# Retention and latent-attention decoder on one core: unused filler tiles that give all matmul operands the same byte offset modulo 512

## The chip, the cores and the metric

The kernel runs on one core of one Trainium2 chip. The metric is device time in microseconds (us) for one execution, as the median of several runs. A core has five engines that run their own instruction streams: TensorE (PE, matmuls and transposes), VectorE (DVE), ScalarE (ACT), GpSimd (POOL) and SyncE (SP, which issues most transfers). The on-chip memory, SBUF, has 128 partitions; a tile takes the same stretch of bytes in every partition, so a tile's place is one byte offset. Matmul results go to PSUM, which has eight banks of 128 x 512 float32.

## The reference

Two layers act on x, 512 tokens of width 1024, in float32. Layer A is a retention layer of 4 heads (key width 256, value width 512), layer B a latent attention of 16 heads (128 plain and 64 rotary query columns, value width 128) on a compressed key and value stream. Both are gated and end in a DeepNorm step:

```python
# layer A: q, k, v, gate = x @ w_in ; rope(q), rope(k) ; o = retention(q, k, v)
# y = (layer_norm(o) * silu(gate)) @ w_out ; x = LayerNorm(alpha * x + y)
# layer B: lat = rms_norm(x @ w_down) ; k, v = lat @ w_up ; q = rms_norm(x @ w_q_lat) @ w_uq
# o = causal_softmax_attention(q, k, v) ; y = (o * silu(x @ w_gate)) @ w_out
# x = LayerNorm(alpha * x + y)
```

## The kernel before

**Arithmetic.** Every float32 operand is split into a high and a low float32r part (`split`, L83 to L85; for weights L49 and L51), and every product is made of three matmuls into one PSUM bank (`mm3`, L77 to L81):

```python
(lh, ll), (rh, rl) = l, r
nc.tensor.matmul(ps, lhsT=lh, rhs=rh, start=start, stop=False)   # L79
nc.tensor.matmul(ps, lhsT=lh, rhs=rl, start=False, stop=False)
nc.tensor.matmul(ps, lhsT=ll, rhs=rh, start=False, stop=stop)
```

`lhsT` is the stationary operand: 128 columns of 4 bytes, so 512 bytes of each partition, which a weight load (LDWEIGHTS, shown as engine PEld) puts into the array. `rhs` is the moving operand: mostly 512 columns, 2048 bytes of each partition. Each matmul has a weight load of its own. In rows of the profile a matmul reads `ps<-moving,stationary`.

**Weights.** `Weights` (L33 to L61) streams them in the order of use: a transfer into one of two `wst` buffers, a cast on ScalarE into `whi`, a subtraction on VectorE or GpSimd into `wlo`, four buffers of each, at least two chunks ahead.

**Order of work.** In layer A, for each head: the value product (`proj_v`), scores, the gate product (`gate`), the product of scores and values (`inner`), the output product of the head before (`out_proj`), the next head's q and k (`proj_qk`), the transposes of the head's output. In `token_proj` (values, gate) the weights move and the transposed input `xT` is stationary; in `proj_qk` and `gate_b` it is the other way round. In layer B, after the latents, 8 pairs of heads run through `scores_b`, `head_proj`, `p_transposes`, `attend`, `gate_b`, `out_b`, `values`. The order is written out by hand, and nothing rearranges it.

**Where tiles lie.** A pool hands out addresses in the order in which tiles are first asked for, each rounded up to 32 bytes. Most tiles are multiples of 512 bytes. The exceptions are the few statistics columns (`ln_st`, `ln_mv`, `ln_rs`, `rs_t`: 640 bytes in pool `keep`; `o_st`, `o_mv`, `o_rs`, `rs_t`: 320 bytes in pool `pa`; `sm`: 128 bytes in pool `pb2`) and what lies ahead of `r`. So the offset modulo 512 changes where such a group has been passed:

| tiles that matmuls read | offset mod 512 before |
|---|---|
| `xTh`, `xTl`, `x1h`, `x1l` (transposed input of layer A and B), `ogh`, `ogl` (gated output of layer B), `qnh`, `qnl` (queries) | 192 |
| `whi`, `wlo` (weights), `qh` .. `kl`, `vh`, `vl`, `sTh`, `sTl` (retention), `lat_h`, `lat_l`, `qlt_h`, `qlt_l` (latents), `krp`, `qr`, `knh`, `knl`, `vbh`, `vbl`, `og_last`, `og`, `p`, `latn` | 320 |
| `oTh`, `oTl` (transposed output of a retention head) | 128 |
| `pTh`, `pTl` (transposed probabilities) | 448 |
| `qn`, `krt` (only transposed) | 32 |
| `ident` (the identity of all transposes) | 128 |

Slices of these tiles start at multiples of 512 bytes, but for the 320-column slices of the chunk `ql1`, every second of which is 256 bytes off.

Of the kernel before, what the change touches and what calls it, by code (L numbers as in the profile page):

```python
# [8 lines left out]
F32 = mybir.dt.float32  # L9
# [5 lines left out]
P = 128  # L15
# [10 lines left out]
SCALE_B = (NOPE + ROPE) ** -0.5  # L26
WC = 1024
LN_EPS, RMS_EPS = 1e-5, 1e-6
# Causal block rows packed into three PSUM banks: block i holds (i + 1) * 128 columns.
SC_AT = {3: (0, 0), 2: (1, 0), 0: (1, 384), 1: (2, 0)}  # L30


class Weights:  # L33
    """Streams weight chunks in the order of their use: load, then the exact split
    w = hi + lo into two float32r parts (12 significant bits each)."""

    def __init__(self, nc, stage, parts, ahead):
        self.nc, self.stage, self.parts, self.ahead = nc, stage, parts, ahead
# [25 lines left out]
def trunk_kernel(ctx, tc, a):  # L64
# [4 lines left out]
    keep = ctx.enter_context(tc.tile_pool(name="keep", bufs=1))  # L69
# [19 lines left out]
    def w_a(key, tag, h):  # L89
        return [(f"{tag}{h}", a[key][4 * h + t], 1024) for t in range(4)]  # L90

    # The order of use: next head's q and k come before the last head's output product.
    order = [("qk0", a["w_qk0"][k], 512) for k in range(KX)]
    for h in range(H_A):
        order += w_a("w_v", "v", h) + w_a("w_g", "g", h)
# [28 lines left out]
    for p in range(NP):  # L124
        i, b = 2 * p, 2 * p + 1
# [15 lines left out]
    order += w_bo(NP - 2, 0) + w_bo(NP - 2, 1) + w_bo(NP - 1, 0) + w_bo(NP - 1, 1)  # L141
    W.todo = order

    # ---------------------------------------------------------------- constants and x
    r = keep.tile([P, NT, D], F32, tag="r", name="r")
    xTs = r.rearrange("p a b -> p (a b)")
    xTh = keep.tile([P, KX, S], F32R, tag="xTh", name="xTh")
# [25 lines left out]
        nc.tensor.matmul(ps_w, lhsT=zero[:, :P], rhs=zero, start=True, stop=True)  # L173

    kvg = keep.tile([P, KVL], F32, tag="kvg", name="kvg")
    for k in range(KX):
        load_xT(k)
        if k < 4:
            W.issue()
# [6 lines left out]
        return xTh[:, k, sl], xTl[:, k, sl]  # L186

    def rsqrt(pool, dst, src, mul, eps):
        """dst = (src * mul + eps) ** -0.5 on [P, 1] columns."""
        t = pool.tile([P, 1], F32, tag="rs_t", name="rs_t", bufs=4)  # L190
        nc.vector.tensor_scalar(t, src, float(mul), float(eps), op0=ALU.mult, op1=ALU.add)
        nc.gpsimd.tensor_tensor(out=dst, in0=t, in1=mhalf, op=ALU.pow)  # L192

    def ln_stats(pool, n):
        """Mean and variance of r[n], and (variance + eps) ** -0.5."""
        st = pool.tile([P, 2, 6], F32, tag="ln_st", name="ln_st", bufs=4)
        for hf in range(2):
            nc.vector.bn_stats(st[:, hf, :], r[:, n, hf * 512 : (hf + 1) * 512])  # L198
        mv = pool.tile([P, 2], F32, tag="ln_mv", name="ln_mv", bufs=4)
        nc.vector.bn_aggr(mv, st.rearrange("p a b -> p (a b)"))  # L200
        rs = pool.tile([P, 1], F32, tag="ln_rs", name="ln_rs", bufs=4)
        rsqrt(pool, rs, mv[:, 1:2], 1.0, LN_EPS)
        return mv, rs

    def ln_apply(pool, n, g, b, stats, on_vector):
        """r[n] = LayerNorm(r[n]) * g + b; column halves on VectorE or on ScalarE and Pool."""
        mv, rs = stats
        halves = [slice(hf * 512, (hf + 1) * 512) for hf in range(2)]
        for sl in halves[:on_vector]:
            y = r[:, n, sl]  # L210
            nc.vector.scalar_tensor_tensor(out=y, in0=y, scalar=mv[:, 0:1], in1=g[:, sl], op0=ALU.subtract, op1=ALU.mult)
        for sl in halves[:on_vector]:
            y = r[:, n, sl]
            nc.vector.scalar_tensor_tensor(out=y, in0=y, scalar=rs, in1=b[:, sl], op0=ALU.mult, op1=ALU.add)  # L214
        if on_vector < 2:
            nm = pool.tile([P, 1], F32, tag="ln_nm", name="ln_nm", bufs=4)
            nc.vector.scalar_tensor_tensor(out=nm, in0=mv[:, 0:1], scalar=-1.0, in1=rs, op0=ALU.mult, op1=ALU.mult)
        for sl in halves[on_vector:]:
            y = r[:, n, sl]
            nc.scalar.activation(y, y, AF.Identity, scale=rs, bias=nm)  # L220
            nc.gpsimd.tensor_tensor(out=y, in0=y, in1=g[:, sl], op=ALU.mult)  # L221
            nc.gpsimd.tensor_tensor(out=y, in0=y, in1=b[:, sl], op=ALU.add)  # L222
# [3 lines left out]
        return x1h[:, k, sl], x1l[:, k, sl]  # L226

    def transposed(src, hi, lo, n, k0, nk):
        """Columns of src [128 tokens, nk * 128] onto partitions, split, at block n."""
        ps = bank()  # L230
        for k in range(nk):
            nc.tensor.transpose(out=ps[:, k * P : (k + 1) * P], in_=src[:, k * P : (k + 1) * P], identity=ident)
        sl = slice(n * P, (n + 1) * P)
        split(
            hi[:, k0 : k0 + nk, sl],
            lo[:, k0 : k0 + nk, sl],
            ps[:, : nk * P].rearrange("p (a b) -> p a b", b=P),
        )
# [4 lines left out]
        for c in range(2):  # L243
            transposed(r[:, n, c * 512 : (c + 1) * 512], x1h, x1l, n, 4 * c, 4)

    # ---------------------------------------------------------------- layer A: retention
    with tc.tile_pool(name="pa", bufs=1) as pa:
        cosA = pa.tile([P, S], F32, tag="cosA", name="cosA")
        sinA = pa.tile([P, S], F32, tag="sinA", name="sinA")
# [89 lines left out]
        def inner(h):  # L339
            sh, sl_, at = sT[h]  # L340
            vh, vl = vv[h]
            o = pa.tile([P, NT, DV_A], F32, tag="og", name="og")
            for n in range(NT):
                ps = bank()
                for mb in range(n + 1):
                    c = slice(at[mb] + (n - mb) * P, at[mb] + (n - mb + 1) * P)
                    mm3(ps, (sh[:, c], sl_[:, c]), (vh[:, mb, :], vl[:, mb, :]), mb == 0, mb == n)
                st = pa.tile([P, 6], F32, tag="o_st", name="o_st", bufs=2)
                mv = pa.tile([P, 2], F32, tag="o_mv", name="o_mv", bufs=2)
                rs = pa.tile([P, 1], F32, tag="o_rs", name="o_rs", bufs=2)  # L350
                nc.vector.bn_stats(st, ps)
                nc.vector.bn_aggr(mv, st)
                # gs holds 2 * silu(gate): 0.5 * rsqrt(var + eps) = rsqrt(4 * (var + eps))
                rsqrt(pa, rs, mv[:, 1:2], 4.0, 4.0 * LN_EPS)
                nc.vector.scalar_tensor_tensor(
                    out=o[:, n, :], in0=ps, scalar=mv[:, 0:1], in1=gs[h][:, n, :], op0=ALU.subtract, op1=ALU.mult
                )
                nc.scalar.activation(o[:, n, :], o[:, n, :], AF.Copy, scale=rs)
            og[h] = o

        def transposes(h):
            hi = pa.tile([P, NT, 4, P], F32R, tag="oTh", name="oTh")
            lo = pa.tile([P, NT, 4, P], F32R, tag="oTl", name="oTl")
            for n in range(NT):
                ps = bank()
                for k in range(4):
                    nc.tensor.transpose(out=ps[:, k * P : (k + 1) * P], in_=og[h][:, n, k * P : (k + 1) * P], identity=ident)
                split(
                    hi[:, n, :, :].rearrange("p a b -> p (a b)"),
                    lo[:, n, :, :].rearrange("p a b -> p (a b)"),  # L370
                    ps,
                )
            oT[h] = (hi, lo)
# [11 lines left out]
            else:  # L385
                nc.vector.tensor_tensor(out=dst, in0=dst, in1=ps, op=ALU.add)

        # Head 3 is done with these when its output weights come.
        W.place["o3"] = [(pa, t + "h", t + "l") for t in ("q", "k", "v", "sT")]
        proj_qk(0)  # L390
        for h in range(H_A):
# [30 lines left out]
            if n >= 2:  # L422
                x1_transposes(n - 2)

    # ---------------------------------------------------------------- layer B: latent attention
    pb = ctx.enter_context(tc.tile_pool(name="pb", bufs=1))
    lat_h = pb.tile([P, 4, S], F32R, tag="lat_h", name="lat_h")
    lat_l = pb.tile([P, 4, S], F32R, tag="lat_l", name="lat_l")
# [4 lines left out]
    sinR = pb.tile([P, S], F32, tag="sinR", name="sinR")  # L433
    mask = pb.tile([P, P], F32, tag="mask", name="mask")
    def rope_proj(g):
        """Rotary query parts of four heads: 32 rows per head, first halves and second halves."""
        ps = []
        for _ in range(2):
            wh, wl = W.get(f"r{g}")
# [13 lines left out]
        uv[g] = t  # L453

    def rope_stack(i):
        """Head i's high parts (twice over the partitions) and low parts, as the keys' order asks."""
        t = pb.tile([P, 2, S], F32R, tag="qr", name="qr", bufs=2)
        rows = slice((i % 4) * 32, (i % 4) * 32 + 32)
        for rep in range(2):
            for j in range(2):  # L460
                at = rep * ROPE + j * 32
                nc.scalar.dma_start(t.bitcast(F32)[at : at + 32, :, :], uv[i // 4].bitcast(F32)[rows, j, :, :])
        qr[i] = (t[:, 0, :], t[:, 1, :])
# [35 lines left out]
    with tc.tile_pool(name="pb1", bufs=1) as p1:  # L499
# [99 lines left out]
        for n in range(NT):  # L599
            src = krt[:, n, :, :].rearrange("p a b -> p (a b)")  # L600
            nc.tensor.transpose(out=psk[:, n * P : (n + 1) * P], in_=src, identity=ident)
        # Rotary keys: high parts on partitions 0-63, low parts on 64-127.
        kh2 = pb.tile([P, S], F32R, tag="tmp", name="kh2", bufs=3)
        nc.scalar.copy(kh2, psk)
        nc.vector.tensor_copy(krp[0:64, :], kh2.bitcast(F32)[0:64, :])
# [4 lines left out]
        values(0)  # L610

    p2 = ctx.enter_context(tc.tile_pool(name="pb2", bufs=1))

    def scores_b(i):
        banks = [bank() for _ in range(3)]
# [119 lines left out]
    b2 = p2.tile([P, D], F32, tag="pTl", name="b2")  # L735
    nc.scalar.dma_start(g2, a["ln_g"][1:2, :].broadcast_to([P, D]))
    nc.scalar.dma_start(b2, a["ln_b"][1:2, :].broadcast_to([P, D]))
    # The last two pairs' output products run as one.
    w = [[], []]
    for p in (NP - 2, NP - 1):  # L740
        for half in range(2):
# [17 lines left out]

# [1 line left out]
def _tiles(w, rows, cols):  # L761
    """[K, N] -> [N / cols, K / rows, 128, rows / 128 * cols]: row blocks of 128 side by side."""
    import numpy as np

    k, n = w.shape
# [2 lines left out]


def _constants():  # L770
    """Rotary angles, decays and the causal mask: they depend on shapes alone."""
    import numpy as np

    def angles(half):
# [82 lines left out]
```

## Time and profile before

| | |
|---|---|
| three runs | 966.04, 968.45, 968.87 us, median 968.45 us |
| the profiled execution | span 965.2 us from the first to the last instruction |
| TensorE | busy 949.6 us (98%), 4637 matmuls and transposes |
| TensorE weight loads | busy 793.9 us (82%) |
| VectorE, ScalarE, GpSimd | busy 56%, 35%, 15% |
| transfers | 94.30 MB, mean 98 GB/s |

The profile gives for the profiled execution its span; what the runs add to a span lies around it, and 968.45 - 965.2 = 3.2 us is that and the spread of the runs together. A matmul's duration in a row reaches from its start until its modelled end, which lies beyond the start of the next one, so durations overlap. How fast TensorE goes is read from the distance between the starts of successive matmuls.

### The profile page before, as it was taken

What the parts mean: (1) busy time and instruction counts of PE and PEld (TensorE: products, weight loads), DVE (VectorE), ACT (ScalarE), POOL (GpSimd) and SP (SyncE); (2) the same over time, 40 slices, a digit from 0 to 9 for tenths busy, and PEclk for the clock granted to TensorE, in tenths of its full rate; (3) what the DMA queues carried; (4) which work ended last, traced back from release to release, by engine and by line L of the source; (5) the groups of instructions that cost most, each with busy time, mean ns of one, the idle gap of its engine ahead of it and who ended that gap; (6) DMA issues with size and microseconds to landing.
All of it is one profiled execution on the core that took longest, in us unless ns stands there. A gap on an engine that the chain in (4) does not pass through costs nothing. (4 is left out here: it accounts for less than half of the span.)

```text
span 965.2 us, 11958 instructions
## 1 busy us (share of the span) xinstructions
PE 949.6 (98%) x4637; PEld 793.9 (82%) x4637; DVE 536.8 (56%) x1006; ACT 334.1 (35%) x577; POOL 147.3 (15%) x103
## 2 busy tenths in 40 slices
PE   9899999999999999999999999999999999999996
PEld 6688888888888888888978888888888888888885
DVE  4734635354344536773276657474664747646657
ACT  4333333233222334123434443343333434333531
POOL 1212101110102012112030010010110100101104
PEclk9999999999999999999999999999999999999999
DMA  7732222123223213213224423332233422423222
GB/s 239 268 130 66 88 88 88 65 88 103 73 66 109 88 66 131 88 36 98 83 72 113 133 65 89 109 115 71 66 105 103 106 80 77 112 85 105 86 63 93
DMA packets 31353, 94.30 MB, mean 98 GB/s; under 512 B 4160, under 2 KB 4544, under 8 KB 31296
## 3 DMA queue, kind: packets, MB, share of 16 engines
q1 hardware_dynamic: 27936, 84.10, 27.2%
q10 hardware_dynamic: 3360, 9.44, 4.0%
q8 instruction: 36, 0.59, 0.3%
q14 instruction: 21, 0.17, 0.1%
HBM read 83.03 MB, written 2.10 MB: 88 GB/s over the span
## 5 line engine op out<-in xcount | busy, mean ns | idle before, releaser
L49 ACT CAST whi<-wst 128x1024 fp32r<-128x1024 f32 (+3 forms) x159 | 151.3, 952 | 341.8 <-PE ps L81 157.5
L51 POOL TENSOR_TENSOR wlo<-wst,whi 128x1024 fp32r<-128x1024 f32 (+3 forms) x53 | 113.5, 2142 | 709.2 <-ACT whi L49 673.6
L51 DVE TENSOR_TENSOR wlo<-wst,whi 128x1024 fp32r<-128x1024 f32 (+3 forms) x106 | 119.5, 1127 | 177.9 <-ACT whi L49 177.5
L80 PE MATMUL ps<-wlo,xTh 128*128 128x512 f32 x256 | 101.1, 395 | 1.9 <-POOL wlo L51 1.9
L79 PE MATMUL ps<-whi,xTh 128*128 128x512 f32 x256 | 101.5, 397 | 0.9 <-ACT whi L49 0.9
L81 PE MATMUL ps<-whi,xTl 128*128 128x512 f32 x256 | 101.0, 394 | 0.0
L80 PEld LDWEIGHTS ps<-wlo,xTh 128*128 128x128 f32 x256 | 48.2, 188 | 13.1 <-POOL wlo L51 2.2
L79 PEld LDWEIGHTS ps<-whi,xTh 128*128 128x128 f32 x256 | 48.3, 189 | 12.3 <-ACT whi L49 1.3
L81 PEld LDWEIGHTS ps<-whi,xTl 128*128 128x128 f32 x256 | 48.2, 188 | 11.1
L79 PE MATMUL ps<-qlt_h,whi 128*128 128x512 f32 x144 | 57.1, 397 | 0.0
L81 PE MATMUL ps<-qlt_h,wlo 128*128 128x512 f32 x144 | 56.5, 392 | 0.0
L80 PE MATMUL ps<-qlt_l,whi 128*128 128x512 f32 x144 | 56.4, 392 | 0.0
L633 ACT ACTIVATE p<-ps,sm 128x512 f32<-128x512 f32 (+1 forms) x64 | 33.3, 526 | 64.7 <-DVE sm L630 64.7
L79 PE MATMUL ps<-xTh,whi 128*128 128x512 f32 x128 | 51.3, 401 | 0.0
L79 PE MATMUL ps<-x1h,whi 128*128 128x512 f32 x128 | 51.2, 400 | 0.0
L81 PE MATMUL ps<-xTh,wlo 128*128 128x512 f32 x128 | 50.9, 398 | 0.0
L80 PE MATMUL ps<-xTl,whi 128*128 128x512 f32 x128 | 50.9, 397 | 0.0
L79 PE MATMUL ps<-whi,oTh 128*128 128x512 f32 x128 | 50.8, 397 | 0.0
L81 PE MATMUL ps<-whi,oTl 128*128 128x512 f32 x128 | 50.6, 396 | 0.0
L80 PE MATMUL ps<-wlo,oTh 128*128 128x512 f32 x128 | 50.6, 395 | 0.0
L81 PE MATMUL ps<-x1h,wlo 128*128 128x512 f32 x128 | 50.5, 395 | 0.0
L80 PE MATMUL ps<-x1l,whi 128*128 128x512 f32 x128 | 50.5, 395 | 0.0
(188 smaller groups left out, 2094.9 us busy)
## 6 DMA issues: line engine op xcount, KB each, us to landing
wst<-in_w_v SPq DMA_DIRECT2D x16, 512.0 KB, 3.3
wst<-in_w_g SPq DMA_DIRECT2D x16, 512.0 KB, 3.3
wst<-in_w_ao SPq DMA_DIRECT2D x16, 512.0 KB, 3.3
wst<-in_w_gb SPq DMA_DIRECT2D x16, 512.0 KB, 3.7
qr<-uv ACTq DMA_DIRECT2D x64, 128.0 KB, 2.3
wst<-in_w_bo SPq DMA_DIRECT2D x16, 512.0 KB, 3.7
wst<-in_w_qk SPq DMA_DIRECT2D x12, 512.0 KB, 3.3
wst<-in_w_q SPq DMA_DIRECT2D x16, 384.0 KB, 3.1
```

The costliest lines, as they stand in the source:

```text
L49: nc.scalar.copy(hi[:, :n], st[:, :n])
L51: eng.tensor_tensor(out=lo[:, :n], in0=st[:, :n], in1=hi.bitcast(F32)[:, :n], op=ALU.subtract)
L79: nc.tensor.matmul(ps, lhsT=lh, rhs=rh, start=start, stop=False)
L80: nc.tensor.matmul(ps, lhsT=lh, rhs=rl, start=False, stop=False)
L81: nc.tensor.matmul(ps, lhsT=ll, rhs=rh, start=False, stop=stop)
L633: nc.scalar.activation(pp, ps, AF.Exp, bias=sm[:, qb, 1:2], scale=SCALE_B, accum_out=sm[:, qb, 2:3])
```

## The change

Three tiles are asked for and never used: 96 float32 columns (384 bytes) in pool `keep` between `kvg` and the statistics columns, 48 columns (192 bytes) in pool `pa` ahead of `oTh`, and 96 columns in pool `pb2` ahead of `p`. No instruction names them. The remaining lines of the diff remove comments and docstrings.

```diff
     kvg = keep.tile([P, KVL], F32, tag="kvg", name="kvg")
+    keep.tile([P, 96], F32, tag="fill", name="fill")
     for k in range(KX):
...
         def transposes(h):
+            if h == 0:
+                pa.tile([P, 48], F32, tag="fill", name="fill")
             hi = pa.tile([P, NT, 4, P], F32R, tag="oTh", name="oTh")
...
     p2 = ctx.enter_context(tc.tile_pool(name="pb2", bufs=1))
+    p2.tile([P, 96], F32, tag="fill", name="fill")
```

On all five queues the instructions stand in the same order as before, with the same waits and signals; only addresses differ. All tiles of the first four rows of the table above now lie at 192 modulo 512, with two exceptions: `p`, which is only transposed, lies at 64, and `qn` and `krt`, also only transposed, at 416. `ident` stays at 128, and the odd slices of `ql1` lie at 448. The last tile ends below the end of the partition, as before.

## Rows read from the trace of the kernel before

**Rows 1.** The page: span, busy time of the engine, granted TensorE clock in 40 slices.
```profile
span 965.2 us, 11958 instructions
...
PE 949.6 (98%) x4637; PEld 793.9 (82%) x4637; DVE 536.8 (56%) x1006; ACT 334.1 (35%) x577; POOL 147.3 (15%) x103
...
PEclk9999999999999999999999999999999999999999
```

**Rows 2.** Waits grouped by who waited for whom: total us, times, longest us.
```profile
PE ps L80 <- POOL wlo L51: 1.9, 1, 1.9
...
ACT whi L49 <- PE ps L81: 157.5, 45, 8.7
```

**Rows 3.** Timeline, start us and duration us: a matmul and the next one's weight load.
```profile
300.32 0.39 PE L80 MATMUL ps<-xTl,whi 128*128 128x512 f32 x1
300.32 0.19 PEld L81 LDWEIGHTS ps<-xTh,wlo 128*128 128x128 f32 x1
```

**Rows 4.** Timeline of TensorE, operands at different offsets: first and last of four unbroken stretches.
```profile
58.66 0.39 PE L80 MATMUL ps<-wlo,xTh 128*128 128x512 f32 x1
...
80.50 0.39 PE L81 MATMUL ps<-whi,xTl 128*128 128x512 f32 x1
...
189.26 0.39 PE L79 MATMUL ps<-xTh,whi 128*128 128x512 f32 x1
...
211.42 0.39 PE L81 MATMUL ps<-xTh,wlo 128*128 128x512 f32 x1
...
268.59 0.40 PE L79 MATMUL ps<-whi,oTh 128*128 128x512 f32 x1
...
290.76 0.39 PE L81 MATMUL ps<-whi,oTl 128*128 128x512 f32 x1
...
557.80 0.39 PE L79 MATMUL ps<-x1h,whi 128*128 128x512 f32 x1
...
563.14 0.40 PE L81 MATMUL ps<-x1h,wlo 128*128 128x512 f32 x1
```

**Rows 5.** Timeline of TensorE, operands at equal offsets: first and last of `inner`, head 0.
```profile
80.72 0.39 PE L79 MATMUL ps<-vh,sTh 128*128 128x512 f32 x1
...
87.30 0.39 PE L81 MATMUL ps<-vh,sTl 128*128 128x512 f32 x1
```

**Rows 6.** Timeline of TensorE, equal offsets after a break: `head_proj` of layer B.
```profile
599.31 0.39 PE L80 MATMUL ps<-qlt_l,whi 128*128 128x512 f32 x1
...
601.39 0.39 PE L80 MATMUL ps<-qlt_l,whi 128*128 128x512 f32 x1
...
602.98 0.39 PE L81 MATMUL ps<-qlt_h,wlo 128*128 128x512 f32 x1
```

**Rows 7.** Groups by line and shape, the first of three lines of each: count, busy us, mean ns.
```profile
L79 PE MATMUL ps<-whi,xTh 128*128 128x512 f32 x256 | 101.5, 397 | 0.9 <-ACT whi L49 0.9
...
L79 PE MATMUL ps<-qlt_h,whi 128*128 128x512 f32 x144 | 57.1, 397 | 0.0
...
L79 PE MATMUL ps<-xTh,whi 128*128 128x512 f32 x128 | 51.3, 401 | 0.0
L79 PE MATMUL ps<-x1h,whi 128*128 128x512 f32 x128 | 51.2, 400 | 0.0
...
L79 PE MATMUL ps<-whi,oTh 128*128 128x512 f32 x128 | 50.8, 397 | 0.0
...
L79 PE MATMUL ps<-whi,ogh 128*128 128x512 f32 x112 | 44.8, 400 | 0.0
...
L79 PE MATMUL ps<-whi,x1h 128*128 128x512 f32 x64 | 25.7, 401 | 0.0
```

**Rows 8.** Busy us of the engines, granted clock (PEclk) and transfers in one stretch.
```profile
480.00:500.00 20.00, 17.94 (x88) 14.73 (x87) 15.27 (x28) 8.53 (x22) 8.39 (x10) 0.91 0.24 70
```

**Rows 9.** Timeline of TensorE: the two rotary score matmuls, and the next one's start.
```profile
564.06 0.40 PE L625 MATMUL ps<-krp,qr 128*128 128x512 f32 x1
...
564.53 0.34 PE L79 MATMUL ps<-knh,qnh 128*128 128x384 f32 x1
```

## The prediction, as put on record

> **What bounds the kernel now.** I first read the page [rows 1]: TensorE is busy 949.6 of 965.2 us, and its granted clock is full in all 40 slices. Other engines can matter only where TensorE waits for them, and the waits by group show next to nothing of that: the largest wait of TensorE is one of 1.9 us, for the low part of a weight chunk [rows 2]. The other way round ScalarE stands 157.5 us in total with its cast of the next chunk until TensorE has finished with a weight buffer [rows 2], so weights come early. Time can therefore only go where TensorE's own stream of matmuls goes faster or slower.
>
> For that stream busy time says nothing, since rows overlap. The timeline does. While a matmul runs, the weights of the next one are loaded: both begin at 300.32 [rows 3], so the moving operand of one matmul and the stationary operand of the next are read at the same time. I therefore sort the 512-column matmuls by the distance, modulo 512 bytes, between what moves and what is loaded meanwhile, with the table of offsets, and take start-to-start distances over unbroken stretches:
>
> - weights moving, xT loaded, 384 apart: 58.66 to 80.50 in 94 steps, 232.3 ns each [rows 4];
> - xT moving, weights loaded, 128 apart: 189.26 to 211.42 in 95 steps, 233.3 ns;
> - weights moving, oT loaded, 320 apart: 268.59 to 290.76 in 95 steps, 233.4 ns;
> - x1 moving, weights loaded, 128 apart, in layer B: 557.80 to 563.14 in 23 steps, 232.2 ns;
> - values moving, scores loaded, both at 320, distance 0: 80.72 to 87.30 in 29 steps, 226.9 ns [rows 5].
>
> 512 columns at 2.4 GHz are 213.3 ns, so each step pays something beyond the columns: about 13.5 ns at distance 0 and about 19 to 20 ns at any other. The stretch at distance 0 follows its neighbour directly, in the same head, with the same shapes and the same clock. What differs is the distance.
>
> A second thing is to be seen. Equal offsets do not give the short step at once. After a break (narrower matmuls, transposes) `head_proj` takes 599.31 to 601.39 for 9 steps, 231.1 ns each, and only then 601.39 to 602.98 for 7 steps, 227.1 ns each [rows 6]. It looks like a pattern that settles and then holds. The stretches at other distances are up to 95 steps long and do not settle.
>
> **The change part by part.** *The three tiles themselves* add no instruction, wait or transfer; they cost memory alone, and nothing is moved past any queue. Zero.
>
> *The stretches whose distance becomes 0.* Each group of [rows 7] stands for three lines (L79 to L81). Taking the price of its own kind of stretch against 226.9:
>
> - weights moving, xT: 3 x 256 = 768 at 5.4 ns, 4.1 us;
> - xT moving, weights: 3 x 128 = 384 at 6.4 ns, 2.5 us;
> - weights moving, oT: 384 at 6.5 ns, 2.5 us;
> - x1 moving, weights: 384 at 5.3 ns, 2.0 us;
> - weights moving, ogh/ogl: 3 x 112 = 336 at 5.4 ns, the price of the first line, which has the same distance of 384, 1.8 us;
> - weights moving, x1: 3 x 64 = 192 at 5.4 ns, 1.0 us;
> - 96 in short stretches of 3 (plain scores against the queries, probabilities against the values): 5 ns as an estimate from the others, 0.5 us.
>
> Together 14.4 us on 2544 matmuls. The 848 other 512-column matmuls (432 with qlt among them) have distance 0 already and give nothing. For 384 columns and fewer, and for the transposes, I take zero: half of the latter keep unequal offsets, and steps this short are not seen to differ.
>
> *What is given back.* First, settling: by [rows 6] a settling costs 9 x (231.1 - 226.9) = 0.04 us. In layer B some 35 of the stretches counted above begin after a break (16 gate products, 14 output products, a few in the latents), so 35 x 0.04 = 1.4 us. From below it is nothing, from above twice that. Second, the first product of the kernel waits for its input and weights to arrive until about 18 us; of its 96 steps some 50 cannot go faster: 50 x 6.4 = 0.3 us. The cover of all weights behind it is the 157.5 us for which ScalarE waits; 13 us spread over the kernel does not use it up. The 1.9 us wait [rows 2] follows a buffer that TensorE itself frees, so it shifts along.
>
> *The clock.* Between 480 and 500 us TensorE is busy 17.94 of 20 us, at a mean clock of 0.91 [rows 8], around a wait for VectorE's query latents. At half clock for 18% of 20 us, 3.6 us, this loses 1.8 us. The wait's chain runs through TensorE's own products, so I expect both to stay; that this stretch escapes the low clock would be worth another 1.8 us, and a second such stretch would cost as much.
>
> **Sum:** 14.4 - 1.4 - 0.3 = 12.7 us. Against the profiled execution: 965.2 - 12.7 = 952.5 us of span. The three runs' median stands 3.2 us above that span, so 968.45 - 12.7 = 955.7 us, rounded to 955.5. Bounds of this case: 14.4 + 1.8 = 16.2 us at best (952.2) and, with twice the settling and a further 1.8 us of low clock, 9.5 us at worst (959).
>
> **The rivals.**
>
> *Offsets do not matter to TensorE; the short steps of distance 0 have another cause.* This kernel would stay at 968.5 us. Against it: besides [rows 5], latents and queries settle at 227 too [rows 6], with other tiles and in another layer. For it: every short step that I can show has both operands at 320, none at 192. The Trainium skill holds this view: "TensorE: Matmul & The Clock Gate", in the steps of Part 2, says that the moving operand and the weight load have read ports of their own, so that loading the next weights takes no read bandwidth from the running matmul. By that rule the distance would change nothing and the result would be 968.5; the steps of 226.9 against 232 to 233 ns speak against it here.
>
> *Distance 0 is needed, but not enough.* The pairs of xT with weights have never been seen at distance 0. If something above the 512 bytes (which part of the memory a tile lies in) keeps them from settling, the first two lines, 6.6 us, fall away with their part of the front end: gain 6.4 us, 962 us.
>
> *Slower: the unsettled pattern stays.* Equal offsets have a slow form as well: the two rotary score matmuls, both operands at 320, take 564.06 to 564.53, 235 ns each [rows 9]. If with all tiles at one offset the stream held on to that form instead of settling, 848 matmuls would go from 226.9 to 235 (+6.9 us) and 2544 from about 232.6 to 235 (+6.1 us): 981 us. The mean step now is about (848 x 226.9 + 2544 x 232.6) / 3392 = 231.2 ns, so this case is slower by 0.3% (2.9 us) from a mean of 232.1 on. Against it: settled stretches are followed by settled ones, and 29 steps held.
>
> *The change does nothing it says:* excluded, the offsets in the built program are those of the change.
>
> **How the numbers follow.** What a measurement of this kernel can tell from no change is about 0.3%, 2.9 us; the three runs before spread by that much. Forecast 0.78; distance 0 not enough for xT 0.11; no effect 0.07; slower 0.04. The forecast's own bounds are 952.2 to 959; to hold 8 times in 10 with some room I reach to the second rival, 951.5 to 962. Faster by over 0.3%: 0.78 + 0.11 = 0.89; within 0.3%: 0.07; slower: 0.04.
>
> **What would show it.** In the changed kernel the value product of head 1 at about 58 us should take 94 steps of 227 ns, 21.3 us instead of 21.8; out_proj and proj_qk 21.5 instead of 22.2 us; `inner` the same 6.6 us as now. TensorE's busy time should fall by as much as the span, to about 937 us, with its list of waits as short as before and ScalarE still waiting for TensorE. The forecast is wrong if steps of xT with weights stay at 232 or more, if `inner` gets longer, or if steps do fall to 227 but new waits of TensorE take the time back.

## The result and the profile after

The changed kernel takes 954.91 us, the median of four runs (951.79 to 955.28), against 968.66 us for the kernel before (966.04 to 970.05): a ratio of 0.9857, 95% interval 0.9841 to 0.9872. That is 13.8 us less; the forecast was 955.5 us. The execution with the profile took 954.98 us, 953.2 us of it span, against 965.2 [rows 1].

The page of the changed kernel, the lines that answer to [rows 1]:

```profile
span 953.2 us, 11958 instructions
...
PE 936.1 (98%) x4637; PEld 793.2 (83%) x4637; DVE 535.3 (56%) x1006; ACT 334.4 (35%) x577; POOL 147.6 (15%) x103
```

The same number of instructions, TensorE busy 13.5 us less, the other engines as before within 2 us. The timeline of TensorE in the changed kernel, the stretches of [rows 4] and then [rows 5] (start us, duration us):

```profile
59.70 0.39 PE L80 MATMUL ps<-wlo,xTh 128*128 128x512 f32 x1
...
81.00 0.39 PE L81 MATMUL ps<-whi,xTl 128*128 128x512 f32 x1
...
187.48 0.39 PE L79 MATMUL ps<-xTh,whi 128*128 128x512 f32 x1
...
209.02 0.40 PE L81 MATMUL ps<-xTh,wlo 128*128 128x512 f32 x1
...
265.18 0.39 PE L79 MATMUL ps<-whi,oTh 128*128 128x512 f32 x1
...
286.71 0.39 PE L81 MATMUL ps<-whi,oTl 128*128 128x512 f32 x1
...
549.46 0.40 PE L79 MATMUL ps<-x1h,whi 128*128 128x512 f32 x1
...
554.70 0.39 PE L81 MATMUL ps<-x1h,wlo 128*128 128x512 f32 x1
...
81.23 0.39 PE L79 MATMUL ps<-vh,sTh 128*128 128x512 f32 x1
...
87.80 0.39 PE L81 MATMUL ps<-vh,sTl 128*128 128x512 f32 x1
```

The steps are 21.30 us / 94 = 226.6 ns (the gate product of head 0), 21.54 / 95 = 226.7, 21.53 / 95 = 226.6, 5.24 / 23 = 227.8 (it begins after a break) and, unchanged, 6.57 / 29 = 226.6. What was 232 to 233 ns is now the step that only `inner` and the latents had.

Something was also given back. TensorE's waits by group, the whole list of those over 1 us:

```profile
PE ps L235 <- DVE qn L569: 2.2, 1, 2.2
PE ps L79 <- ACT whi L49: 2.1, 2, 1.8
PE ps L80 <- POOL wlo L51: 1.9, 1, 1.9
PE ps L173 <- DVE zero L170: 1.2, 1, 1.2
```

In the second group 1.8 us are new: the profile of before has 0.9 us there, one wait at 30 us. The new wait lies in the first product, and behind the third line's wait a stretch at half clock (1.2 GHz) follows, 0.42 us from start to start, which the profile of before does not have there:

```profile
18.23 0.50 PE L79 MATMUL ps<-xTh,whi 128*128 128x512 f32 x1 [1.77 <-ACT whi L49]
...
32.41 0.76 PE L80 MATMUL ps<-wlo,xTh 128*128 128x512 f32 x1 [1.92 <-POOL wlo L51]
...
33.39 0.63 PE L79 MATMUL ps<-whi,xTh 128*128 128x512 f32 x1
33.81 0.63 PE L80 MATMUL ps<-wlo,xTh 128*128 128x512 f32 x1
```

The matmul at 32.41 did not come earlier than before the change, though the steps ahead of it are shorter. Its line, and the cast of the chunk that it waits for, before and then after:

```profile
32.45 0.50 PE L80 MATMUL ps<-wlo,xTh 128*128 128x512 f32 x1 [1.93 <-POOL wlo L51]
28.92 1.04 ACT L49 CAST whi<-wst 128x1024 fp32r<-128x1024 f32 x1 [5.06 <-PE ps L80]
...
28.88 1.05 ACT L49 CAST whi<-wst 128x1024 fp32r<-128x1024 f32 x1 [4.89 <-DMA wst<-in_w_v]
```

Before, the cast began when TensorE had finished with a buffer; now it begins when the chunk has landed.

Sums over all start-to-start distances of 512-column float32r steps, less 226.7 ns each, make the account of the two profiled executions. A step counts as equal when what moves and what is loaded for the next matmul lie at the same place modulo 256. Steps at unequal offsets lost 14.9 us before and 0.1 now; equal ones, which are longer while they settle after a break, 1.2 before and 2.1 now; steps over 260 ns (waits, breaks, half clock) 13.7 before and 15.0 now, of which the first 40 us have 6.8 and 8.8. Together 14.8 - 0.9 - 1.3 = 12.6 us less; the spans differ by 12.0 us, the rest lies in narrower matmuls and at the end.

### The profile page after: what moved, and what is told of

Same layout as the page of the kernel before. It is cut to its first block, busy times and chain, and to the rows that moved or that the text cites. A ratio compares the mean times of both kernels' runs of the same rounds, so it can differ in the third digit from the quotient of the medians.

```text
span 953.2 us, 11958 instructions
## 1 busy us (share of the span) xinstructions
PE 936.1 (98%) x4637; PEld 793.2 (83%) x4637; DVE 535.3 (56%) x1006; ACT 334.4 (35%) x577; POOL 147.6 (15%) x103
```

## The experiments

**One row of 32 distances, nothing else on the engines.** In place of the kernel, 48 matmuls at each distance, moving and stationary operand read from two constant tiles (the lines shortened):

```diff
+    for d in range(0, 512, 16):
+        for j in range(48):
+            s = j % 4
+            nc.tensor.matmul(ps, lhsT=st[:, d//4 + s*128 : d//4 + (s+1)*128],
+                             rhs=mv[:, s*512 : (s+1)*512], start=True, stop=True)
```

> This kernel computes nothing of the reference: after 64 matmuls to warm up it runs 48 matmuls of 512 float32r columns at each of 32 distances between the moving and the loaded operand, 0 to 496 bytes in steps of 16, with nothing else on the engines, in the order of the distances. Theory A (only equal offsets modulo 512 let TensorE fall into the short step): 227 ns a step at distance 0, 231 to 234 ns at each of the other 31. Rival B (the distance is not the cause, something else in the full kernel is): one and the same step at all 32 distances. Rival C (a smaller period counts, of which the kernel before happened to show only bad values, 128, 320 and 384): 227 ns at several distances, 64 or 256 among them.

The timeline of TensorE in this kernel, merged rows (start, time from the first start to the last end, count), at distances 0, 16, 48, 96 and 256:

```profile
28.11 10.59 PE L57 MATMUL apart<-mv,st 128*128 128x512 f32 x46
...
38.99 10.59 PE L57 MATMUL apart<-mv,st 128*128 128x512 f32 x46
...
61.08 10.90 PE L57 MATMUL apart<-mv,st 128*128 128x512 f32 x46
...
94.59 10.94 PE L57 MATMUL apart<-mv,st 128*128 128x512 f32 x46
...
205.94 10.59 PE L57 MATMUL apart<-mv,st 128*128 128x512 f32 x46
```

Less the last matmul's 0.39 us, 45 steps are 226.7, 226.7, 233.6, 234.4 and 226.7 ns. Distance is here and below the place of what is loaded less the place of what moves. The step by distance, as a mean of the last 20 in each stretch, the stretches in order of distance without a break:

| distance, bytes | 0, 16, 240 | 32 to 64 | 80 | 96 | 112 to 160 | 176 | 192 | 208, 224 |
|---|---|---|---|---|---|---|---|---|
| ns | 226.7 | 233.3 | 232.0 | 234.3 | 233.3 to 233.4 | 230.0 | 228.9 | 233.3 |
| 256 further | 226.7 | 233.3 | 232.0 | 234.2 | 233.3 to 233.4 | 230.0 | 228.8 | 233.3 |

So the distance alone makes the difference, with no other engine at work, and the second half repeats the first: over these 512 bytes the period is 256 and not 512 (rival C). The kernel before had 128, 320 (64 beyond 256) and 384 (128 beyond), all three where the step is 233.3 ns. The values at 16 and 240 depend on what ran before, as two further kernels show below.

**Only the first filler.**

```diff
-            if h == 0:
-                pa.tile([P, 48], F32, tag="fill", name="fill")
-    p2.tile([P, 96], F32, tag="fill", name="fill")
```

> Only the first of the three fillers; all tiles at 192 but oTh and oTl (0) and pTh and pTl (320). Theory A: the 384 matmuls with oT stay at 233 ns (2.5 us) and 48 short ones with pT (0.2 us), the rest as in the changed kernel: 957.5 us, out_proj in 22.2 us and proj_qk in 21.5 us for 95 steps. Rival B: no change in either direction that goes with a group of tiles; the gain is lost or kept as a whole (955 or 968 us).

956.47 us, ratio 0.988 (0.9865 to 0.9895), 1 us under theory A. Timeline of TensorE, first and last of `out_proj` of head 0 in this kernel:

```profile
165.06 0.40 PE L79 MATMUL ps<-whi,oTh 128*128 128x512 f32 x1
...
187.23 0.39 PE L81 MATMUL ps<-whi,oTl 128*128 128x512 f32 x1
```

22.17 us as before the change, 233.4 ns a step, while the product right behind it, xT with weights, runs at 227.0 ns. The gain goes tile by tile with the offsets.

**All operands at 0 instead of 192.**

```diff
+    keep.tile([P, 80], F32, tag="shift", name="shift")
     r = keep.tile([P, NT, D], F32, tag="r", name="r")
```

> The changed kernel with another filler of 320 bytes ahead of r, so that all operands lie at 0 modulo 512 instead of 192; distances stay 0. Theory A: the same time as the changed kernel, 955 us, steps of 226.7 ns. Rival D (the place itself counts, 192 is a good one): another time, up to 968 us.

954.1 us, ratio 0.985 (0.9825 to 0.9876), long stretches at 226.7 ns: between these two places there is no difference.

**256 apart.** The first filler is `[P, 32]` instead of `[P, 96]`.

> The first filler is 128 bytes instead of 384, so that xT, x1, ogh and qnh lie at 192 and all other operands at 448: a distance of 256 where the kernel before had 128 or 384, and 0 for oT and pT. Theory A: only oT and pT gain, 2.7 us: 966 us, steps of 232 to 233 ns for xT with weights. Rival C with a period of 256: as the changed kernel, 955 us, steps of 227 ns throughout.

953.58 us, ratio 0.9849 (0.9826 to 0.9872), the stretch of xT with weights (q and k of head 2) at 226.7 ns a step. In the whole kernel too, equal modulo 256 is enough; theory A in its form of 512 falls.

**96 apart.** The first filler is `[P, 120]`.

> The first filler is 480 bytes instead of 384: the operands of 2064 matmuls of 512 columns (xT, x1, ogh, qnh with weights and keys) lie 96 apart, the distance with the longest step in the row of 32 (234.2 ns), those of oT and pT 0 apart. Theory A with the steps of that row: 2064 x (234.2 - 226.7) = 15.5 us over the changed kernel less what the first product does not pass on, so 969 to 970 us: slower than the kernel before or level with it. Rival (the gain comes from the fillers in some other way, such as what else they move): 955 us.

966.82 us, ratio 0.9987 (0.9975 to 1.0): the gain is gone although all three fillers are there. It came out 2 to 3 us under the expectation, and the account says where. The distance has a sign, which the expectation left out: where xT moves and weights are loaded it is 96, and 742 such steps took 234.1 ns; where weights move and xT is loaded it is -96, that is 160, and 1315 such steps took 233.4 ns. Together they lost 14.3 us where 15.5 was reckoned. And the steps over 260 ns in the first 40 us are 5.8 us, 3.0 us fewer than in the profile of the changed kernel. That a slower TensorE runs less into the weights' arrival is not shown by this: a second profile of the changed kernel has 6.3 us there.

**Which of two reads has to match.** A second kernel of stretches; places alternate by 64 bytes so that either the next weights (those loaded meanwhile) or the own weights (those of the same matmul) lie 0 apart from what moves (the places written out; first the moving one, then the stationary one):

```diff
+    steps(48, lambda j: 64 * (j % 2), lambda j: 64 * ((j + 1) % 2))   # next weights 0 apart
+    steps(48, lambda j: 64 * (j % 2), lambda j: 64 * (j % 2))         # own weights 0 apart
```

> Computes nothing of the reference: after a warm-up, stretches of 48 steps with nothing else on the engines. Theory A (what counts is the distance, modulo 256 bytes, between the operand that moves and the weights that are loaded for the next matmul): with places that alternate by 64 bytes so that moving and next loaded are 0 apart and moving and own weights 64 apart, 227 ns; the other way round 233 ns. Rival (the own weights count): 233 and 227. Fine distances of 4 to 16 bytes 227 ns, and by 28 near 233. Equal distances at other places (64, 132) as at 0. For 384, 256 and 128 columns and for transposes: theory A gives no number; if the two reads meet only while 512 columns run against a load of 128, 120 ns at 256 columns and 110 ns at 128 columns whatever the distance. After a break of transposes or narrow steps: at distance 0 some 5 to 10 longer steps before the short one, at 64 and 128 never the short one.

Merged rows of its timeline, the two alternating stretches, then both operands 132 bytes past the start of their tiles:

```profile
29.34 10.90 PE L59 MATMUL ps<-mv,st 128*128 128x512 f32 x46
...
40.54 10.82 PE L59 MATMUL ps<-mv,st 128*128 128x512 f32 x46
...
140.62 11.16 PE L59 MATMUL ps<-mv,st 128*128 128x512 f32 x46
```

233.6, 231.8 and 239.3 ns: neither match is enough by itself, which none of the expectations had. The rest of this kernel: distances of 4 to 28 bytes 230.0 to 235.0 ns, so not the smooth edge that was expected, and 16 among them 233.3 where the first row has 226.7 right behind distance 0; moving at 192 and loaded at 0, a distance of 64, 233.3 ns, the other way round 229.1; 384 columns 173.3 ns at 0 and 192, 176.7 at 64, 176.0 at 128; 256 columns 120.0 ns at 0 and 117.8 to 118.7 at the others; 128 columns 111.5 to 111.7 and transposes 109.2 ns at any. After a break, distance 0 needed 9 or 10 longer steps three times and none once, then held 226.7; 240 came to it once in four times; 4, 8, 16, 64, 128 and 252 never did.

**Entry and place.** A third kernel of stretches (the lines shortened; `settle` is 32 steps at distance 0):

```diff
+    for by in (32, 64, 128, 256): steps(48, flips(0, by), flips(1, by))   # next weights always 0 apart
+    for _ in range(3): steps(12, at(0), at(0)); steps(12, at(64), at(64))
+    for v in (4, 8, 16, 32, 64, 128, 256): settle(); steps(48, at(v), at(v))
+    for d in (4, 8, 16, 32, 252, 240, 224, 64): settle(); steps(48, at(0), at(d))
```

> Computes nothing of the reference: stretches of 48 steps of 512 float32r columns with nothing else on the engines. First the moving place alternates by 32, 64, 128 or 256 bytes from step to step while the weights loaded for the next step always lie 0 apart from it. Theory A2 (both the own and the next weights have to be 0 apart from what moves, modulo 256): 227 ns only where it alternates by 256. Rival A1 (the next weights alone): 227 ns at all four. Then blocks of 12 steps at one place and 12 at another, 64 apart, operands equal within a block: A2 says 227 ns within a block after a few longer steps at its start. Then equal places 4 to 256 bytes past a 512-byte step: 227 ns where the place is a multiple of 16, more (239 ns at 132) where it is not. Then distances of 4 to 252 entered from the settled pattern: held at 16 (226.8 ns in the row of 32, where it followed distance 0) though not reached from a break (233 ns after transposes), lost at 32 and 64. Last bfloat16 at distances 0 to 192: if the short step is one in which the two reads do not meet, bfloat16 with half the bytes has a shorter one and depends less on the distance; no number.

Merged rows, the moving place alternating by 64, 128 and 256:

```profile
47.96 10.90 PE L64 MATMUL ps<-mv,st 128*128 128x512 f32 x46
...
66.46 10.75 PE L64 MATMUL ps<-mv,st 128*128 128x512 f32 x46
...
84.78 10.59 PE L64 MATMUL ps<-mv,st 128*128 128x512 f32 x46
```

233.6 (as at 32, 233.3), 230.2 and 226.7 ns: only places that are equal modulo 256 from step to step keep the short step, as A2 says, and A1 falls. In blocks of 12 with a shift of 64 between them, the steps after each shift are long again, 10 at 64 bytes and 3 on the way back. Both operands 4, 8 and 16 bytes past the start of their tiles give 239.2, 232.8 and 230.0 ns, 32, 64, 128 and 256 bytes past it 226.7. The expectation for multiples of 16 was wrong. Distances of 16, 240 and 252 hold the short step if it is running when they begin, though 16 and 252 did not reach it from a break; 4, 8, 32, 64 and 224 lose it. bfloat16 takes 215.8 ns at distances 0 to 128.

**What was given back at the front.** The loads of x and of three rows of constants held back by one-column copies that depend on the first value product:

```diff
+                for t in (g1, b1, qg):
+                    nc.vector.tensor_copy(t[:, 0:1], vv[0][0].bitcast(F32)[:, 0, 0:1])
...
+                    nc.vector.tensor_copy(r[:, n, 0:1], vv[0][0].bitcast(F32)[:, n, 0:1])
                     nc.sync.dma_start(r[:, n, :], a["x"][:, n, :])
```

> The changed kernel, with the loads of x, of the norm's rows and of q_norm (7 transfers, 3.4 MB) held back until the first value product has run, so that they no longer stand between the weight chunks of the first 30 us (7 one-column copies on VectorE hold them). Theory F (the changed kernel gives back about 2 us in its first 40 us, because TensorE now waits there for weights and then runs a stretch at half clock): the first value chunk comes some 2 to 5 us earlier, the wait of 1.9 us at 30 us and the half clock behind it go: 951 us, 3 to 4 us below the changed kernel. Rival (these loads do not delay the weights): 955 us as the changed kernel.

952.54 us (952.17 to 952.92), ratio 0.9838 (0.982 to 0.9855): 2.4 us below the changed kernel where 3 to 4 were expected, and by another way than was said. In its profile there is no half clock between 20 and 40 us, but the wait of 1.9 us at 30 us stands as it was.

**A product in the place of a wait.**

```diff
         q_transposes(2)
+        head_proj(0, "k")
         q_transposes(3)
-        head_proj(0, "k")
```

> The changed kernel, with the key product of head 0 put ahead of the last of the four query transposes of layer B: 2.7 us of matmuls in the place of the wait of 2.2 us for VectorE's last query latent at about 481 us, which is followed by half clock. If both go: 2.2 + 1.6 = 3.8 us, 951 us; if the wait only moves behind the transposes (the query product needs their split), under 1 us: 954 us.

954.17 us (950.99 to 955.1), ratio 0.9849 (0.9827 to 0.9871): not to be told from the changed kernel. The wait of 2.2 us is replaced by two of 0.4 and 0.8 us for the split of the transposes, and the clock from 470 to 500 us is 1.00 where it was 0.94; but the profiled execution, one of the longer ones, had a mean clock of 0.83 between 20 and 40 us.

**Both edits.**

> Both edits. If they add up: 947 to 948 us, ratio to the kernel before 0.978; no stretch at half clock but the first few us. If the low clock is a matter of chance in either place, between that and 951 us.

952.01 us (949.85 to 954.01), ratio 0.9832 (0.9809 to 0.9856): 1 us above even the second of the two outcomes. In its profile the clock is 1.00 from 470 to 500 us but 0.91 from 20 to 40 us: the stretch at half clock that the first edit was to remove is there again.

**The changed kernel again, and a third edit beside it.**

> The changed kernel once more, to stand beside the next one on the same chip: 955 us, ratio to the kernel before 0.986.

955.42 us (952.81 to 955.96), ratio 0.9866 (0.9851 to 0.9881).

```diff
-        eng = nc.gpsimd if self.n % 3 == 2 else nc.vector
+        eng = nc.gpsimd if self.n % 3 == 2 and self.n != 8 else nc.vector
```

> The two edits of f3_both, and the low part of the first value chunk (the ninth chunk) on VectorE instead of GpSimd, which takes 2.1 us where VectorE takes 1.1 us. If the wait of 1.9 us at 30 us is GpSimd's subtraction, it shrinks by 1 us or more, the stretch at half clock behind it comes less often, and the median is 949 to 951 us; if VectorE is held up there by the rotary step, 952 us as f3_both.

950.25 us (949.15 to 950.91), ratio 0.9817 (0.9804 to 0.983), beside 955.42 on the same chip, and no run of one reaches into those of the other. The wait of 1.9 us at 30 us is now one of 0.8 us, so it was GpSimd's subtraction:

```profile
30.27 0.49 PE L80 MATMUL ps<-wlo,xTh 128*128 128x512 f32 x1 [0.76 <-DVE wlo L51]
```

Busy times by stretch, with the granted clock behind them, in this kernel, then in the changed kernel beside it, then in the changed kernel's first profile:

```profile
20.00:40.00 20.00, 19.23 (x84) 15.37 (x83) 11.44 (x14) 7.13 (x8) 2.30 (x1) 1.00 0.56 176
465.00:500.00 35.00, 33.38 (x186) 28.73 (x185) 22.16 (x40) 12.98 (x31) 9.99 (x11) 1.00 0.28 86
...
20.00:40.00 20.00, 18.08 (x79) 14.46 (x78) 10.54 (x14) 6.39 (x7) 2.89 (x2) 1.00 0.80 275
465.00:500.00 35.00, 32.76 (x171) 28.08 (x171) 21.75 (x40) 13.11 (x31) 9.95 (x11) 0.95 0.27 86
...
20.00:40.00 20.00, 17.77 (x70) 14.05 (x69) 11.36 (x14) 6.38 (x7) 2.64 (x3) 0.91 0.81 272
```

84 matmuls in the same 20 us, against 79 in the changed kernel at full clock and 70 in its profile with the half clock. This version is the best of the study.

## Why the prediction was right

**Steps.** The term of 14.4 us for 2544 matmuls was read off rows of the kernel before and came out as 14.8 us. The stretch named as a test, 94 steps in 21.3 us, takes 21.30 (it is the gate product of head 0, ScalarE's tanh follows it; the prediction calls it the value product of head 1); `inner` is unchanged as foretold; TensorE is busy 936.1 us where about 937 was said.

**Settling.** 1.4 us was taken; the account has 0.9 us more than before. The reading of [rows 6] held: the pattern after a break is longer, then settles and stays.

**The front and the clock.** This is the mis-sized term. The prediction took 0.3 us for the first product's arrival and said that TensorE's list of waits would stay as short. In the profiled execution a wait of 1.8 us at 18 us is new, and so is the half clock behind 32 us; the first 40 us gave back 2.0 us. The 1.9 us wait was to follow a buffer that TensorE frees, and so to shift along; it ended at 32.45 us before and at 32.41 now, since the chunk's landing had taken the place of the buffer, and its length is GpSimd's subtraction. All this varies: in a second profile of the same kernel, with a span of 951.0 us, that first wait is 0.7 us and the clock from 20 to 40 us is 1.00. Of eight runs of the changed kernel two took 951.8 and 952.8 us and six 954.9 to 956.0; the two profiles are one of each kind. What decides whether the clock falls there is open, since the same 1.9 us wait has half clock behind it in some profiles and not in others. The three edits of the last version, at the front and at 481 us, took another 5.2 us off the changed kernel (955.42 to 950.25), clock included. The page's row of PEclk, which the prediction first read as full in all slices, could not show this: its digit 9 stands for 90% or more of a slice of 24 us, and it is 9 in all 40 slices of the changed kernel too.

**The sum.** That 12.7 us and 955.5 us came out so near is partly luck. Against the account the gain of the steps was put 0.4 us too low, the price of settling 0.5 too high and that of the front 1.7 too low (2.0 instead of 0.3), and behind 40 us the waits and breaks, put at nothing, gave 0.7 back: 12.6 together. The span fell by 12.0 us and the medians by 13.8, because the profiled execution of before was one of its shorter ones: the time lies 1.8 us above the span, not 3.2, in the profiled execution of the changed kernel (954.98 and 953.2).

**The condition.** The prediction sorted by distance modulo 512 and by the pair of what moves and what is loaded next. It was enough for the sum, since the change makes everything equal, but both were only part: the period is 256, and the places have to stay the same, modulo 256, from step to step.

**The rivals.** *Offsets don't matter* falls with the row of distances. The Trainium skill's rule that it was named with ("TensorE: Matmul & The Clock Gate", Part 2, on independent read ports), read as there (the distance changes nothing), is not what float32r shows here, 226.7 against 233.3 ns with nothing else running; for bfloat16 no stretch from 0 to 128 bytes contradicts it. *Not enough for xT* falls with 226.6 and 226.7 ns for these pairs. *Slower, the unsettled pattern stays* falls: the settled one held over 95 steps. The pair of [rows 9], 235 ns each at equal offsets behind unequal ones, takes 555.60 to 556.06 us now, 230 ns each.

**The order.** "Nothing rearranges it", said of the order of work, holds for TensorE. On SyncE's queue it does not: there the loads of `decay` and x stand ahead of weight chunks that come earlier in the code. In the kernel before:

```profile
14.00 1.38 SPq L395 DMA_DIRECT2D decay<-in_decay  x3
18.10 2.76 SPq L45 DMA_DIRECT2D wst<-in_w_qk  x2
```

## What to carry to other kernels

Where TensorE is the bound and its operands are float32r with 512 columns to a matmul, take the distance from start to start of successive matmuls, not their durations, and set it against columns over the clock; if stretches of equal shape differ by 2 to 3%, look at the byte offsets of their tiles. Small tiles that shift what is allocated behind them are the cause to look for, and padding them so that the tiles behind lie at equal places modulo 256 bytes costs only memory. Then look at where TensorE now arrives early: a wait that was covered may begin to cost (1.8 us at 18 us here), and a stretch at half clock may follow.

## What the runs showed of the hardware that was not expected

- The step of 512 float32r columns depends on the distance between what moves and what is loaded, with a period of 256 bytes over the 512 tried: 226.7 ns when they are equal, 228.8 to 234.3 ns at the multiples of 16 but 16 and 240. At 384 columns the step is 173.3 ns at 0 and 192, 176.0 and 176.7 at 128 and 64. At 256 and 128 columns and for transposes no gain of equal places is seen (120.0 against 117.8 to 118.7, 111.7 and 109.2 ns).
- The short step is a state. Once running it survives distances of 16, 240 and 252 bytes. After a break or a change of place it comes back within some 10 steps where both operands lie at equal places that are multiples of 32 bytes; from a break it came at a distance of 240 in one of four tries, at 4, 8, 16, 64, 128 and 252 never.
- bfloat16 goes at 215.8 ns and float32r at best at 226.7, 11 ns more for the same columns. The Trainium skill ("TensorE: Matmul & The Clock Gate", "Wait — 56ns, not 53.3ns?") gives 215.7 ns for 512 columns, measured; the bfloat16 stretches agree, the float32r ones never reach it.
- Why the distance counts, and why a constant place is needed from step to step, no run here settles.
